# Stores of new keys on ScalarE's queue, forget sums on GpSimd's, temporaries moved, and a softmax that takes the minimum of negated scores

## The chip, the cores and the metric

The kernel runs on one core of a Trainium2 chip. The metric is the time of one execution on the device in microseconds (us). The engines are named as in the profile: PE is TensorE, and PEld its weight loads; DVE is VectorE, ACT ScalarE, POOL GpSimd and SP SyncE. SyncE only issues transfers here; ScalarE and GpSimd issue some between their own instructions. An engine works through its instructions in the order in which they were placed, and an instruction that waits holds all that stand behind it.

## The reference

One inference step of a two-layer trunk for 512 prompt rows and 8 x 16 sample rows (640 rows in all, model width 1024, branch width 2048). Layer 0 is a gMLP layer that the change does not touch. Layer 1 is attention with 16 heads of 128 and a forget gate:

```python
proj = h @ w_in                               # q, k, v, z and 16 forget columns
logf = log_sigmoid(proj[..., 4 * E:] + b_f)
# prompt: causal, for each head
cT = cumsum(logf, axis=1)
s = q @ k.T * scale + cT[query] - cT[key]     # then the causal mask
o = softmax(s) @ v
# sample: the same over 256 cached rows (cache_fox_k, cache_fox_v, cache_fox_logf) and 16 new ones
y = (o * silu(z)) @ w_out
```

After it come an RMS norm, the residual and a gated embedding, as in layer 0. The new k, v and logf rows of prompt and sample are outputs too, in the layout (row, head, channel).

## The kernel before, in words

Products in float32 are made of three products of float32r parts: `split(hi, lo, src)` (line 285) rounds on ScalarE (line 288) and takes the rest on VectorE (line 289), and `mm3` (line 269) issues the three matmuls (lines 271 to 273). The projections of layer 1 use a scheme of seven products for a 2 x 2 block (`seven_products`, line 556): of each product of 12 matmuls, into one of four PSUM banks (`PRJ` and `UZ`), the first is copied out by ScalarE (line 571) and the others are added out by VectorE (lines 562, 573, 575, 578). The left operands are sums of weight blocks that GpSimd builds (line 210), and GpSimd also issues the weights' loads. The right operands are sums of blocks of h that `right_operands` makes on VectorE (lines 426 to 437).

The heads are worked through in pairs p = 0 to 7. While TensorE projects z of pair p and v, k, q of pair p + 1, the attention of pair p is cut into pieces that `interleave(steps, pieces)` (line 356) puts between the matmuls: each matmul step adds an estimated time, and each piece has a due time. The attention pieces use three other banks (`ATT`). The compiler's planner then orders each engine's instructions by a simulated timeline, so that a due time is a wish and not a place; `queued("dve")` ties the instructions inside it behind the last one that was noted in `behind`.

What the pieces do, by the names that matter here:

- `forget_logits` (line 808), `log_forget` (line 820) and `forget_sums` (line 840) make the 16 forget columns, their log sigmoid and its cumulative sums for all heads, once, at the start of the layer. The sums are stored to DRAM (`c_sc` for the prompt, `cs_sc` for the samples) and read back as a row that is spread over 128 partitions: `load_w0(h)` for a head's prompt row (into `SF` or `CST`), `load_mask(i)` for four sample requests.
- `load_k(p, bg, hh)` (line 1039) loads the cached K of a head and four requests into the one buffer `kraw` with four transfers of 1024 pieces of 128 bytes. `turn_k` (line 1051) turns it with four VectorE transposes (line 1055), after which the next load may start; `new_k` adds the new keys. `load_v` loads cached V.
- `prompt_pieces(h)` (line 974): `scores(i)` takes scores of a block of 128 queries, subtracts the forget row, takes the row maximum in the same VectorE instruction (lines 1004 and 1007), negates it (line 1010), and ScalarE takes the Exp (line 1011); then `turn` (line 1022) and `values` (line 1029), whose last step writes y over z (line 1031). `sample_pieces` does the same for four requests (lines 1079 to 1120), its negation in line 1084.
- `store_k(h, tr)` (line 919) transposes a head's new keys on VectorE and stores them with eight transfers in pieces of 128 bytes, on SyncE's queue. It is called from `project_k` when a head's sum is done, for both heads of a pair in close sequence.
- `store_y(p)` (line 1138) stores both heads' y on GpSimd's queue at the end of a pair; the next pair's z is written to the same place, the odd head first.

Before the loop over pairs stand `project_v0`, `project_k0` and `project_q(0)` for the first pair, with the forget gate's pieces and the first loads between them. The forget gate's temporaries lie in one run from the start of `R1` (`tmpa`), over the buffers of turned K (`o_KT`) and raw K (`o_K`).

Of the kernel before, what the change touches and what calls it, by code (L numbers as in the profile page):

```python
# [24 lines left out]
P = 128  # L25
# [32 lines left out]
def hybrid_trunk(tc, x_prompt, x_sample, ck, cv, clf, p_prompt, p_sample, norm_pre, norm_post,  # L58
# [31 lines left out]
    def r1(o, n, p=P):  # L90
        return R1[:p, o:o + n]
# [191 lines left out]
    scale = DH ** -0.5  # L283
# [495 lines left out]
    def tmpa(n, p=P):  # L779
        nonlocal o  # L780
        res = r1(o, n, p)
        o += n
        return res
# [11 lines left out]
    cr = tmpa(256).rearrange("p (t n) -> p t n", t=2)  # L795
# [6 lines left out]
    fx, fa, fe, fl, fu, lft = (tmpa(n) for _ in range(6))  # L802
    lf3 = lft.rearrange("p (t h) -> p t h", t=NT)
    fx3 = fx.rearrange("p (t h) -> p t h", t=NT)
    cT, ex, cS = tmpa(SEQ, H), tmpa(P), tmpa(272)
    assert o <= o_V
# [33 lines left out]
    def forget_sums():  # L840
# [4 lines left out]
        dma(c_sc, cT)  # L845
# [9 lines left out]
        dma(cs_sc, cS)  # L855
# [63 lines left out]
    def store_k(h, tr):  # L919
        nc.vector.transpose(out=tr, in_=both(o_k, h % 2))  # L920
        trv = tr.rearrange("p (c d) -> p c d", d=32)
        for qd in range(4):
            dma(fk_p[0, 0, :, h, qd * 32:(qd + 1) * 32].rearrange("(c j) d -> j c d", j=32), trv[qd * 32:(qd + 1) * 32, :16])
            dma(fk_s[0, :, :, h, qd * 32:(qd + 1) * 32].rearrange("(c b) q d -> (b q) c d", c=4), trv[qd * 32:(qd + 1) * 32, 16:])

    def project_k0():
        ws = weights(2)
        n = TOK - SA
        for h in range(2):
# [4 lines left out]
            nc.vector.tensor_tensor(out=kt[:, SA:], in0=kt[:, SA:], in1=b[:, :n], op=ALU.add)  # L934
# [39 lines left out]
    def prompt_pieces(h):  # L974
# [13 lines left out]
        def scores(i):  # L988
# [12 lines left out]
            init = -3e38  # L1001
            if i:
                m0 = small()
                nc.vector.tensor_tensor_reduce(out=pr[:, :i * P], in0=S[:, :i * P], in1=w0[:, :i * P], scale=1.0, scalar=init,
                                               op0=ALU.subtract, op1=ALU.max, accum_out=m0)
                init = m0
            nc.vector.tensor_tensor_reduce(out=pr[:, d], in0=S[:, d], in1=w1, scale=1.0, scalar=init,
                                           op0=ALU.subtract, op1=ALU.max, accum_out=m)
            nm, sm = small(), small()
            nc.vector.tensor_scalar(out=nm, in0=m, scalar1=-1.0, scalar2=None, op0=ALU.mult)  # L1010
            nc.scalar.activation(out=pr[:, :n], in_=pr[:, :n], func=AF.Exp, bias=nm, accum_out=sm)  # L1011
# [54 lines left out]
    def sample_pieces(p, bg):  # L1066
# [6 lines left out]
        def scores():  # L1073
# [3 lines left out]
            for hh in range(2):  # L1077
                for bl in range(4):
                    nc.tensor.matmul(S[32 * bl:32 * bl + 32, :272], qpads[:, hh, 4 * bg + bl].rearrange("p h q -> p (h q)"),  # L1079
                                     kt[:, hh, bl], start=(hh == 0), stop=(hh == 1))  # L1080
            m, nm, sm, ri = small(), small(), small(), small()
            nc.vector.tensor_tensor_reduce(out=pr[:, :272], in0=S[:, :272], in1=Wc, scale=1.0, scalar=-3e38, op0=ALU.subtract,
                                           op1=ALU.max, accum_out=m)
            nc.vector.tensor_scalar(out=nm, in0=m, scalar1=-1.0, scalar2=None, op0=ALU.mult)
            nc.scalar.activation(out=pr[:, :272], in_=pr[:, :272], func=AF.Exp, bias=nm, accum_out=sm)
# [52 lines left out]
    def store_y(p):  # L1138
        for hh in range(2):
            dma(y_sc[2 * p + hh], y_of(2 * p + hh), nc.gpsimd)  # L1140
# [13 lines left out]
    def attention_pieces(p, step, s1):  # L1154

        s0, t0 = 5, 4
        pieces = sample_times(p, 0, s0) + sample_times(p, 1, s1)
        pieces += [(s0 + 5, lambda: turn_k(p, 1, 0)), (s0 + 5.1, lambda: load_k(p, 1, 1)), (s0 + 17.6, lambda: turn_k(p, 1, 1)),
                   (s0 + 17.7, lambda: new_k(p, 1)), (s0 + 13.5, lambda: load_v(p, 1))]
        for hh in range(2):  # L1160
            pieces += prompt_times(2 * p + hh, t0 + 4 * step * hh, step)
        if p < 7:
            pieces += [(s0 + 17.8, lambda: load_k(p + 1, 0, 0)), (s1 + 13.5, lambda: load_v(p + 1, 0))]
# [11 lines left out]
    def sums_of_h():  # L1175
        sums.append(right_operands((o_P, o_v + 1280, o_V, o_qp, o_z)))

    interleave(project_v0(), [(0.0, forget_logits), (0.1, sums_of_h), (6.0, log_forget)])
    interleave(project_k0(), [(1.0, forget_sums), (4.0, lambda: load_k(0, 0, 0)), (6.0, lambda: load_w0(0)), (6.05, lambda: load_w0(1)), (6.06, lambda: load_mask(0)), (6.1, lambda: load_v(0, 0))])
    split(*quarter(0, 1), sums[0])  # L1180
    nc.gpsimd.memset(r1(o_qp, 512), 0.0)
    interleave(project_q(0), [(0.2, lambda: turn_k(0, 0, 0)), (0.3, lambda: load_k(0, 0, 1)), (12.0, lambda: turn_k(0, 0, 1)),
                              (12.1, lambda: load_k(0, 1, 0)), (12.2, lambda: new_k(0, 0))])
# [49 lines left out]
```

## Time and profile before

| | |
|---|---|
| Time, median of 3 runs | 1314.44 us (1314.06 to 1314.46) |
| The profiled execution's own time | 1318.47 us |
| Its span, first to last instruction | 1316.6 us |
| PE busy | 1286.0 us (98%) |
| DVE, ACT, POOL busy | 970.5 us (74%), 587.8 us (45%), 349.1 us (27%) |
| Mean share of the DMA queue of SyncE (q1) | 35.5% of 16 engines |
| GpSimd's queue (q0), ScalarE's queue (q10) | 13.7%, 1.2% |

Matmuls are pipelined, so that "busy" hides what a slow clock costs; the granted clock (PEclk, 1.00 is full speed) has to be read beside it. The attention layer's projections begin at 531.5 us of the span; the last pair's z projection ends near 1111 us, and the output projection follows. In a timeline row stand the start, the duration (us), engine, line, operation, what is written and read, the number of merged instructions, and in brackets how long the engine was idle before it and what ended that. "SPq" and "ACTq" rows are issues of transfers by SyncE and ScalarE; their duration is the time in which that engine's sequencer was held.

### The profile page before, as it was taken

How to read it: one execution, taken by the hardware profiler on the slowest of the kernel's cores; microseconds unless marked ns; L12 is line 12 of the kernel's file. 1: busy time of each engine (PE TensorE's matmuls, PEld its weight loads, DVE VectorE, ACT ScalarE, POOL GpSimd, SP SyncE). 2: the span in 40 equal slices, each digit the busy share in tenths (PEclk: the TensorE clock that was granted, in tenths of full speed). 3: DMA queues.
4: the chain of work that ended last, by engine and by line, in shares of the span. 5: the costliest groups of instructions: out<-in, count | busy, mean ns of one | idle time of the engine just before them, and what ended most of it. 6: DMA issues, size and time to landing. Idle time of an engine off the chain costs nothing. (4 is left out here: it accounts for less than half of the span.)

```text
span 1316.6 us, 21174 instructions
## 1 busy us (share of the span) xinstructions
PE 1286.0 (98%) x7873; PEld 1147.1 (87%) x7873; DVE 970.5 (74%) x1888; ACT 587.8 (45%) x1062; POOL 349.1 (27%) x322
## 2 busy tenths in 40 slices
PE   9999999999999999998989999999989999999998
PEld 6888999999988888886878999999979998788887
DVE  7744999999844455986858888889879987744643
ACT  5334555444535343453435444544444444535431
POOL 1012454543000100343432444444434530000100
PEclk9999999999999999998999999999989999999999
DMA  6432333232324213457878768677778757742111
GB/s 226 131 108 67 122 119 118 91 99 73 129 96 154 70 49 108 123 112 144 154 148 161 182 160 180 150 167 141 153 117 187 170 118 205 283 140 80 65 57 56
DMA packets 275545, 171.53 MB, mean 130 GB/s; under 512 B 188721, under 2 KB 238689, under 8 KB 275442
## 3 DMA queue, kind: packets, MB, share of 16 engines
q1 hardware_dynamic: 261770, 128.63, 35.5%
q0 software_dynamic: 9760, 36.05, 13.7%
q10 hardware_dynamic: 3912, 5.50, 1.2%
q8 instruction: 62, 1.02, 0.3%
q14 instruction: 41, 0.34, 0.1%
HBM read 148.55 MB, written 21.59 MB: 129 GB/s over the span
## 5 line engine op out<-in xcount | busy, mean ns | idle before, releaser
L271 PE MATMUL pb<-A,W 128*128 128x320 f32 (+1 forms) x752 | 242.4, 322 | 7.2 <-DVE R L578 3.7
L273 PE MATMUL pb<-A,W 128*128 128x320 f32 (+1 forms) x752 | 236.3, 314 | 0.0
L272 PE MATMUL pb<-A,W 128*128 128x320 f32 (+1 forms) x752 | 235.3, 313 | 0.0
L271 PE MATMUL pb<-W,A 128*128 128x512 f32 x520 | 204.9, 395 | 3.5 <-DVE R L562 2.0
L272 PE MATMUL pb<-W,A 128*128 128x512 f32 x520 | 203.7, 392 | 0.0
L273 PE MATMUL pb<-W,A 128*128 128x512 f32 x520 | 203.3, 393 | 0.1
L289 DVE TENSOR_TENSOR W<-RAW,W 128x1024 fp32r<-128x1024 f32 (+1 forms) x126 | 144.8, 1150 | 74.2 <-ACT W L288 71.8
L288 ACT ACTIVATE W<-RAW 128x1024 fp32r<-128x1024 f32 (+1 forms) x126 | 119.9, 952 | 94.8 <-PE pb L273 48.3
L271 PEld LDWEIGHTS pb<-A,W 128*128 128x128 f32 x752 | 143.4, 191 | 9.3 <-DVE R L578 4.0
L272 PEld LDWEIGHTS pb<-A,W 128*128 128x128 f32 x752 | 143.3, 191 | 1.2 <-issue 0.9
L273 PEld LDWEIGHTS pb<-A,W 128*128 128x128 f32 x752 | 143.0, 190 | 0.8 <-issue 0.4
L271 PEld LDWEIGHTS pb<-W,A 128*128 128x128 f32 x520 | 98.1, 189 | 23.9 <-ACT A L288 2.3
L301 POOL TENSOR_TENSOR SML<-SML 128x1 f32<-128x1 f32 x25 | 18.5, 740 | 376.9 <-DVE SML L299 372.2
L271 PE MATMUL pb<-tbf,W 128*128 128x320 f32 x360 | 117.5, 326 | 0.1
L273 PEld LDWEIGHTS pb<-W,A 128*128 128x128 f32 x520 | 97.9, 188 | 20.6 <-DVE A L289 0.5
L272 PEld LDWEIGHTS pb<-W,A 128*128 128x128 f32 x520 | 98.0, 188 | 19.6
L210 POOL TENSOR_TENSOR sff<-RAW 128x512 f32<-128x512 f32 x46 | 60.8, 1322 | 202.8 <-DVE W L289 97.6
L272 PE MATMUL pb<-tbf,W 128*128 128x320 f32 x360 | 112.2, 312 | 0.0
L273 PE MATMUL pb<-tbf,W 128*128 128x320 f32 x360 | 112.0, 311 | 0.0
L562 DVE TENSOR_TENSOR R<-R,pb 128x320 f32<-128x320 f32 x184 | 86.6, 479 | 20.1 <-PE pb L273 13.6
L289 DVE TENSOR_TENSOR A<-R,A 128x640 fp32r<-128x640 f32 (+1 forms) x42 | 34.5, 854 | 61.9 <-ACT A L288 61.9
L1011 ACT ACTIVATE R<-R,SML 128x128 f32<-128x128 f32 (+1 forms) x64 | 35.7, 558 | 92.5 <-DVE SML L1010 91.9
(267 smaller groups left out, 2875.2 us busy)
## 6 DMA issues: line engine op xcount, KB each, us to landing
RAW<-in_fox_w_in POOLq DMA_DIRECT2D x46, 512.0 KB, 7.2
RAW<-in_gmlp_w_in SPq DMA_DIRECT2D x40, 512.0 KB
R<-in_cache_fox_v SPq DMA_DIRECT2D x32, 512.0 KB
R<-in_cache_fox_k SPq DMA_DIRECT2D x128, 128.0 KB
RAW<-in_gmlp_w_out SPq DMA_DIRECT2D x16, 512.0 KB
RAW<-in_ple_w_gate SPq DMA_DIRECT2D x16, 512.0 KB
RAW<-in_fox_w_out SPq DMA_DIRECT2D x16, 512.0 KB
R<-in_fox_w_in POOLq DMA_DIRECT2D x14, 512.0 KB, 7.7
```

Source lines behind the costliest of these rows:

```text
L210: nc.gpsimd.tensor_tensor(out=o, in0=a, in1=b, op=op)
L271: nc.tensor.matmul(out, lh, rh, start=start, stop=False)
L272: nc.tensor.matmul(out, lh, rl, start=False, stop=False)
L273: nc.tensor.matmul(out, ll, rh, start=False, stop=stop)
L288: nc.scalar.activation(out=hi, in_=src, func=AF.Copy)
L289: nc.vector.tensor_tensor(out=lo, in0=src, in1=f(hi), op=ALU.subtract)
L301: nc.gpsimd.tensor_tensor(out=q, in0=t, in1=mhalf, op=ALU.pow)
L562: behind["dve"] = nc.vector.tensor_tensor(out=into(i, j), in0=a, in1=b, op=ALU.add)
L1011: nc.scalar.activation(out=pr[:, :n], in_=pr[:, :n], func=AF.Exp, bias=nm, accum_out=sm)
```

## The change

The forget row is added to negated scores and the minimum is taken (the scale of q is negative now); the Exp gets scale -1 and the minimum as its bias, and the instruction that negated the maximum falls away, in `scores` of prompt and sample. The new keys are stored over ScalarE's queue. The sums of the forget gate are stored, and the first rows loaded, over GpSimd's queue. Its temporaries move to other buffers, so that raw K's buffer is free from the start of the layer and the first load of cached K is issued in `project_v0`; the order and due times of the first pieces change with it. y is stored head by head, the even head's at a due time inside the pair. The prompt pieces begin at 3.2 instead of 4, and in pairs 0 to 6 follow in steps of 4.7 instead of 4.8. `project_k0` notes its VectorE sum in `behind`.

```diff
-    scale = DH ** -0.5
+    scale = -DH ** -0.5
...
-    cr = tmpa(256).rearrange("p (t n) -> p t n", t=2)
+    cr = r1(o_PTs + 96, 256).rearrange("p (t n) -> p t n", t=2)
...
-    fx, fa, fe, fl, fu, lft = (tmpa(n) for _ in range(6))
+    fx, fa, fe, fl, fu, lft = (r1(o_V + 1280 + z * n, n) for z in range(6))
...
-    cT, ex, cS = tmpa(SEQ, H), tmpa(P), tmpa(272)
-    assert o <= o_V
+    cT, ex, cS = r1(o_PT + 288, SEQ, H), r1(o_PT + 800, P), r1(o_V + 1760, 272)
+    assert o <= o_K and o_PT + 288 >= o_P + 1280 and o_PTs + 96 >= o_qp + 1280
...
-        dma(c_sc, cT)
+        dma(c_sc, cT, nc.gpsimd)
...
-        dma(cs_sc, cS)
+        dma(cs_sc, cS, nc.gpsimd)
...
         for qd in range(4):
-            dma(fk_p[0, 0, :, h, ...], trv[qd * 32:(qd + 1) * 32, :16])
-            dma(fk_s[0, :, :, h, ...], trv[qd * 32:(qd + 1) * 32, 16:])
+            dma(fk_p[0, 0, :, h, ...], trv[qd * 32:(qd + 1) * 32, :16], nc.scalar)
+            dma(fk_s[0, :, :, h, ...], trv[qd * 32:(qd + 1) * 32, 16:], nc.scalar)
...
-            nc.vector.tensor_tensor(out=kt[:, SA:], in0=kt[:, SA:], in1=b[:, :n], op=ALU.add)
+            behind["dve"] = nc.vector.tensor_tensor(out=kt[:, SA:], in0=kt[:, SA:], in1=b[:, :n], op=ALU.add)
...
-            init = -3e38
+            init = 3e38
             if i:
                 m0 = small()
                 nc.vector.tensor_tensor_reduce(out=pr[:, :i * P], in0=S[:, :i * P], in1=w0[:, :i * P], scale=1.0, scalar=init,
-                                               op0=ALU.subtract, op1=ALU.max, accum_out=m0)
+                                               op0=ALU.add, op1=ALU.min, accum_out=m0)
...
-            nm, sm = small(), small()
-            nc.vector.tensor_scalar(out=nm, in0=m, scalar1=-1.0, scalar2=None, op0=ALU.mult)
-            nc.scalar.activation(out=pr[:, :n], in_=pr[:, :n], func=AF.Exp, bias=nm, accum_out=sm)
+            sm = small()
+            nc.scalar.activation(out=pr[:, :n], in_=pr[:, :n], func=AF.Exp, scale=-1.0, bias=m, accum_out=sm)
...
-    def store_y(p):
-        for hh in range(2):
-            dma(y_sc[2 * p + hh], y_of(2 * p + hh), nc.gpsimd)
+    def store_y(h):
+        dma(y_sc[h], y_of(h), nc.gpsimd)
...
-        s0, t0 = 5, 4
+        s0, t0 = 5, 3.2
...
         if p < 7:
-            pieces += [(s0 + 17.8, lambda: load_k(p + 1, 0, 0)), (s1 + 13.5, lambda: load_v(p + 1, 0))]
+            pieces += [(s1 + 18, lambda: store_y(2 * p)), (s0 + kb + 0.2, lambda: load_k(p + 1, 0, 0)), (s1 + 13.5, lambda: load_v(p + 1, 0))]
...
-    interleave(project_v0(), [(0.0, forget_logits), (0.1, sums_of_h), (6.0, log_forget)])
-    interleave(project_k0(), [(1.0, forget_sums), (4.0, lambda: load_k(0, 0, 0)), (6.0, lambda: load_w0(0)), (6.05, lambda: load_w0(1)), (6.06, lambda: load_mask(0)), (6.1, lambda: load_v(0, 0))])
+    interleave(project_v0(), [(0.0, forget_logits), (2.0, log_forget), (2.1, sums_of_h), (9.0, forget_sums),
+                              (9.1, lambda: load_w0(0, nc.gpsimd)), (1.0, lambda: load_k(0, 0, 0))])
+    interleave(project_k0(), [(11.0, lambda: turn_k(0, 0, 0)), (11.1, lambda: load_k(0, 0, 1)), (0.0, lambda: load_w0(1, nc.gpsimd)), (0.1, lambda: load_mask(0, nc.gpsimd)), (6.0, lambda: load_v(0, 0))])
     split(*quarter(0, 1), sums[0])
     nc.gpsimd.memset(r1(o_qp, 512), 0.0)
-    interleave(project_q(0), [(0.2, lambda: turn_k(0, 0, 0)), (0.3, lambda: load_k(0, 0, 1)), (12.0, lambda: turn_k(0, 0, 1)),
-                              (12.1, lambda: load_k(0, 1, 0)), (12.2, lambda: new_k(0, 0))])
+    interleave(project_q(0), [(8.0, lambda: turn_k(0, 0, 1)),
+                              (8.1, lambda: load_k(0, 1, 0)), (12.2, lambda: new_k(0, 0))])
...
-        pieces = attention_pieces(p, 4.8, 26.0) + next_keys(p + 1, 34.0, 46.2)
+        pieces = attention_pieces(p, 4.7, 26.0) + next_keys(p + 1, 34.0, 46.2)
...
-        store_y(p)
+        store_y(2 * p + 1)
```

The sample scores change like the prompt's.

More of the change, by code (lines that the diff above doesn't have):

```diff
@@ L922, in store_k @@
         for qd in range(4):
-            dma(fk_p[0, 0, :, h, qd * 32:(qd + 1) * 32].rearrange("(c j) d -> j c d", j=32), trv[qd * 32:(qd + 1) * 32, :16])
-            dma(fk_s[0, :, :, h, qd * 32:(qd + 1) * 32].rearrange("(c b) q d -> (b q) c d", c=4), trv[qd * 32:(qd + 1) * 32, 16:])
+            dma(fk_p[0, 0, :, h, qd * 32:(qd + 1) * 32].rearrange("(c j) d -> j c d", j=32), trv[qd * 32:(qd + 1) * 32, :16], nc.scalar)
+            dma(fk_s[0, :, :, h, qd * 32:(qd + 1) * 32].rearrange("(c b) q d -> (b q) c d", c=4), trv[qd * 32:(qd + 1) * 32, 16:], nc.scalar)
     def project_k0():
@@ L1004, in scores @@
                 nc.vector.tensor_tensor_reduce(out=pr[:, :i * P], in0=S[:, :i * P], in1=w0[:, :i * P], scale=1.0, scalar=init,
-                                               op0=ALU.subtract, op1=ALU.max, accum_out=m0)
+                                               op0=ALU.add, op1=ALU.min, accum_out=m0)
                 init = m0
             nc.vector.tensor_tensor_reduce(out=pr[:, d], in0=S[:, d], in1=w1, scale=1.0, scalar=init,
-                                           op0=ALU.subtract, op1=ALU.max, accum_out=m)
-            nm, sm = small(), small()
-            nc.vector.tensor_scalar(out=nm, in0=m, scalar1=-1.0, scalar2=None, op0=ALU.mult)
-            nc.scalar.activation(out=pr[:, :n], in_=pr[:, :n], func=AF.Exp, bias=nm, accum_out=sm)
+                                           op0=ALU.add, op1=ALU.min, accum_out=m)
+            sm = small()
+            nc.scalar.activation(out=pr[:, :n], in_=pr[:, :n], func=AF.Exp, scale=-1.0, bias=m, accum_out=sm)
             if i == 3 and h + 2 < 14:
@@ L1080, in scores @@
                                      kt[:, hh, bl], start=(hh == 0), stop=(hh == 1))
[L1081 to L1085, printed above, removed]
+            m, sm, ri = small(), small(), small()
+            nc.vector.tensor_tensor_reduce(out=pr[:, :272], in0=S[:, :272], in1=Wc, scale=1.0, scalar=3e38, op0=ALU.add,
+                                           op1=ALU.min, accum_out=m)
+            nc.scalar.activation(out=pr[:, :272], in_=pr[:, :272], func=AF.Exp, scale=-1.0, bias=m, accum_out=sm)
             if 2 * p + bg < 15:
@@ L1154, in attention_pieces @@
     def attention_pieces(p, step, s1):
-        s0, t0 = 5, 4
+        s0, t0 = 5, 3.2
         pieces = sample_times(p, 0, s0) + sample_times(p, 1, s1)
-        pieces += [(s0 + 5, lambda: turn_k(p, 1, 0)), (s0 + 5.1, lambda: load_k(p, 1, 1)), (s0 + 17.6, lambda: turn_k(p, 1, 1)),
-                   (s0 + 17.7, lambda: new_k(p, 1)), (s0 + 13.5, lambda: load_v(p, 1))]
+        ka, kb = 5, 17.6
+        pieces += [(s0 + ka, lambda: turn_k(p, 1, 0)), (s0 + ka + 0.1, lambda: load_k(p, 1, 1)), (s0 + kb, lambda: turn_k(p, 1, 1)),
+                   (s0 + kb + 0.1, lambda: new_k(p, 1)), (s0 + 13.5, lambda: load_v(p, 1))]
         for hh in range(2):
```

## The prediction, made before the changed kernel ran

> **What bounds the kernel now.** I read the page first: one core, one span, and shares of the engines.
>
> ```profile
> span 1316.6 us, 21174 instructions
> PE 1286.0 (98%) x7873; PEld 1147.1 (87%) x7873; DVE 970.5 (74%) x1888; ACT 587.8 (45%) x1062; POOL 349.1 (27%) x322
> PEclk9999999999999999998999999999989999999999
> ```
>
> TensorE is the bound: it is busy for 98% and the change takes no matmul away. So the change can only win what TensorE loses in the attention layer, which is all that it touches. The second view is the table by windows of 20 us; these are the windows from 560 us on in which TensorE's time, the first number behind the width, is under 20.
>
> ```profile
> core 0: us, PE busy (x) PEld busy (x) DVE busy (x) ACT busy (x) POOL busy (x), PEclk, DMA share, GB/s
> 560.00:580.00 20.00, 19.05 (x118) 17.86 (x118) 18.67 (x28) 11.41 (x17) 9.17 (x8) 1.00 0.44 104
> 580.00:600.00 20.00, 17.45 (x112) 15.43 (x110) 10.66 (x20) 6.34 (x9) 7.42 (x8) 0.98 0.82 160
> 600.00:620.00 20.00, 17.91 (x84) 12.90 (x85) 17.02 (x48) 8.98 (x19) 7.87 (x8) 0.85 0.69 121
> 620.00:640.00 20.00, 18.18 (x140) 16.65 (x139) 17.47 (x49) 9.13 (x20) 7.96 (x8) 1.00 0.62 112
> 660.00:680.00 20.00, 16.24 (x122) 14.81 (x121) 12.52 (x33) 6.75 (x14) 7.96 (x9) 1.00 0.74 160
> 680.00:700.00 20.00, 17.52 (x116) 16.21 (x115) 14.19 (x40) 9.08 (x21) 7.05 (x7) 0.91 0.76 134
> 700.00:720.00 20.00, 18.51 (x144) 17.34 (x143) 16.32 (x47) 9.34 (x20) 6.92 (x7) 1.00 0.82 173
> 960.00:980.00 20.00, 15.02 (x91) 13.74 (x91) 11.89 (x29) 5.52 (x11) 6.52 (x5) 0.83 0.58 84
> 1100.00:1120.00 20.00, 17.97 (x113) 15.20 (x111) 14.29 (x42) 7.86 (x16) 0.47 (x2) 1.00 0.72 189
> 1120.00:1140.00 20.00, 19.16 (x115) 14.50 (x115) 15.27 (x43) 11.74 (x23) 0.00 (x0) 1.00 0.96 356
> ```
>
> Ten windows lack 200 - 177.01 = 22.99 us of TensorE. Behind three of the stalls the granted clock is about half as well, which a third view, windows cut to those stretches, prices: what is lost is the width times what the clock lacks.
>
> ```profile
> 601.20:606.20 5.00, 4.19 (x15) 3.79 (x16) 5.00 (x12) 2.40 (x4) 2.29 (x3) 0.50 0.48 89
> 688.00:691.50 3.50, 3.50 (x16) 3.50 (x15) 2.93 (x8) 0.85 (x2) 2.50 (x3) 0.51 0.07 8
> 972.90:979.40 6.50, 6.50 (x26) 5.75 (x27) 6.50 (x13) 2.54 (x7) 5.48 (x5) 0.59 0.39 60
> ```
>
> 5.00 x 0.50 = 2.5, 3.50 x 0.49 = 1.7, 6.50 x 0.41 = 2.7: another 6.9 us. The pot is 22.99 + 6.9 = 29.9 us. Fourth, TensorE's timeline names the longest stalls in brackets with the releaser, and VectorE's, ScalarE's and SyncE's timelines what lay behind that releaser.
>
> ```profile
> 572.84 0.42 PE L271 MATMUL pb<-A,W 128*128 128x320 f32 x1 [0.60 <-ACT A L288]
> 601.18 0.64 PE L271 MATMUL pb<-A,W 128*128 128x320 f32 x1 [3.73 <-DVE R L578]
> 687.03 0.42 PE L271 MATMUL pb<-A,W 128*128 128x320 f32 x1 [2.48 <-DVE R L562]
> 972.90 0.69 PE L271 MATMUL pb<-W 128*128 128x384 f32 x1 [4.98 <-DVE SML L1007]
> 1112.01 0.47 PE L271 MATMUL pb<-W,A 128*128 128x512 f32 x1 [1.96 <-DVE R L562]
> ...
> 598.51 0.29 DVE L994 TENSOR_TENSOR R<-sff,CST 128x128 f32<-128x128 f32 x1 [7.93 <-DMA sff<-c_sc]
> 663.91 1.43 DVE L1055 STREAM_TRANSPOSE R<-R 128x256 f32<-128x256 f32 x4 [4.40 <-DMA out<-R]
> 686.49 0.49 DVE L562 TENSOR_TENSOR R<-R,pb 128x320 f32<-128x320 f32 x1 [3.93 <-DMA y_sc<-R]
> 946.12 1.42 DVE L1055 STREAM_TRANSPOSE R<-R 128x256 f32<-128x256 f32 x4
> 969.03 1.42 DVE L1055 STREAM_TRANSPOSE R<-R 128x256 f32<-128x256 f32 x4 [8.11 <-DMA R<-in_cache_fox_k]
> ...
> 1105.86 0.74 ACT L288 ACTIVATE A<-R 128x640 fp32r<-128x640 f32 x1 [8.17 <-DMA R<-y_sc]
> ...
> 592.82 8.77 SPq L124 DMA_DIRECT2D R<-in_cache_fox_k  x4
> 930.33 2.46 SPq L124 DMA_DIRECT2D R<-in_cache_fox_k  x4
> 932.89 17.58 SPq L124 DMA_DIRECT2D out<-R  x16
> 951.61 8.31 SPq L124 DMA_DIRECT2D R<-in_cache_fox_k  x4
> 1078.20 8.47 SPq L124 DMA_DIRECT2D out<-R  x16
> ```
>
> The pattern: VectorE takes its work in order and stands before a transfer (the forget sums' first row at 598.51, the cached K at 663.91 and 969.03, the stored y at 686.49); the sums that empty the projections' banks (L562, L578) are queued behind it, and TensorE runs out of banks. At 930 to 960 the cause can be read off SyncE: four loads of cached K take 2.46 us to issue; the 16 stores of new K then hold SyncE for 17.58 us; the next four loads begin at 951.61, need 8.31 us, and land at 969.03.
>
> **The change, part by part.** The profiled execution took 1318.47 us (span 1316.6 and 1.87 around it), 4.03 us above the median of the runs, 1314.44. The sum is made against 1318.47 and the 4.03 taken off.
>
> Forget sums through GpSimd's queue, temporaries moved, logs ahead of the sums of h, first cache loads early. L994 waited for a row that could be stored only after the sums, late in the K projection, and whose load left SyncE's queue shortly before 592.82. The sums now belong into the V projection, which ends some 20 us before 590, where L994 began to wait. The stall of 3.73, its follower of 0.81 in the next window (2.55 + 2.09 = 4.64 with the rest of those two windows) and the half clock's 2.5 go: -7.1. What is late next: VectorE does the logs before the sums of h, whose last split (the row of 0.60 at 572.84) feeds project_q(0), and GpSimd, which builds the weights' left operands (L210), now stands before a transfer's landing at each of its loads. No row shows that wait on GpSimd. Its ends: nothing, if both fill idle time, or the 3.73 of the like stall at 601.18 once more; I take +1.5, nearer to nothing, since VectorE is the only full engine there (18.67 of 20) and the logs are no added work. The first V load now waits for the stored sample sums; no stall row above names a V load, so 0.
>
> Cached K of the first pair. With the temporaries out of its buffer, its load starts before the K projection instead of at 592.82, and each later turn follows. The 1.82 of 620:640 goes: -1.8; if the loads are still late nothing is won.
>
> Stores of new K over ScalarE's queue. SyncE loses 128 issues (eight for each of 16 heads), and the load at 951.61 could leave at once when its buffer is free. Its landing took 969.03 - 951.61 = 17.4 us, of which 8.31 were issue; with an issue like the 2.46 at 930.33 it lands some 6 us earlier, and some 4 more for an earlier start (the VectorE turn that frees the buffer ends at 946.12 + 1.42 = 947.5). The wait of 8.11 is covered: 4.98 + 2.7 = -7.7. For the three windows from 660 to 720, 3.76 + 2.48 + 1.49 = 7.73 and the half clock's 1.7, 9.4 in all, a turn that waits (663.91) began it and a late y store (686.49) ended it; I take two thirds, -6.3. The last two windows, 2.03 + 0.84 = 2.87, hang on y loads queued behind cached K; half, -1.4. Their ends: nothing, and all of it. The first of those ends is the rival of the full DMA engines below.
>
> What ScalarE pays.
>
> ```profile
> L124 SPq DMA_DIRECT2D out<-R x185: 315/486/5832, 134.0 to 1313.2; - x185
> 927.00:950.00 23.00, 23.00 (x172) 21.93 (x171) 19.78 (x47) 10.95 (x19) 8.90 (x10) 1.00 0.73 131
> 578.19 0.31 PE L271 MATMUL pb<-tbf,W 128*128 128x320 f32 x1
> 581.57 0.31 PE L273 MATMUL pb<-tbf,W 128*128 128x320 f32 x1
> ...
> L1010 DVE TENSOR_SCALAR SML<-SML x64: 117/147/160, 600.2 to 1163.9; 128x1 f32<-128x1 f32 x64
> L1084 DVE TENSOR_SCALAR SML<-SML x16: 141/153/155, 627.5 to 1139.1; 128x1 f32<-128x1 f32 x16
> ```
>
> A pair's 16 issues cost 16 x 0.486 = 7.8 us if the queue takes them, up to the 17.58 above if it blocks. Behind them stand the copies of each first product out of its bank (L571), the weights' splits and the Exp. Cover: ScalarE is busy for 10.95 of the 23 us around the stores, so 18.7 with them; and four banks of 12 matmuls at (581.57 - 578.19)/23 = 0.147 us each, 1.76 a product, let TensorE run 3 x 1.76 = 5.3 us on. If all issues stand in front of one copy, 7.8 - 5.3 = 2.5 us show per pair; at 17.58 it would be 12.3; if the order interleaves them, 0. Below nothing is excluded, since the gain on SyncE is counted above. I take +1.0 for each of seven pairs, +7: nearest to the cheap end, because the issues alone leave ScalarE 4 us free of 23 and the stores no longer stand behind loads in one queue.
>
> Minimum of negated scores: 64 x 0.147 + 16 x 0.153 = 11.9 us of VectorE go, and one hop before each Exp. The sign sits in a constant that the split of q's weights multiplies anyway. TensorE does not wait for the Exp in any of the five rows above, so 0; with VectorE at 19.78 of 23 it could be a few us, and its absence costs nothing. y head by head: the same two stores of each pair, the even one earlier; counted in the 1.7 and 7.73 above, else 0; the cover is the three products before the odd head's old y is overwritten. Prompt pieces 0.8 us earlier and steps of 4.7 instead of 4.8: 0, since they shift pieces within a TensorE that is full. Bounds for the shift: one lost or won stall like 1112.01's, +-2.
>
> Sum: -7.1 + 1.5 - 1.8 - 7.7 - 6.3 - 1.4 + 7 = -15.8. 1318.47 - 15.8 = 1302.7; less 4.03: 1298.7, say 1299.
>
> **The rivals.**
>
> Full DMA engines. K loads and K stores wait for the same 16 engines, not for SyncE. For it: the engines' share stands at 0.73 around the stores. Against it: at 0.73 they aren't full, the share falls to 0.58 in the window of the longest stall, and the same 16 stores took 8.47 us at 1078.20. The stalls of 660 to 720, 960 and 1100 stay, ScalarE is hardly stopped (2 in all): -7.1 + 1.5 - 1.8 + 2 = -5.4, 1309. The Trainium skill, DMA: Bandwidth & Descriptors, Issuing engines are not separate DMA queues, speaks for this one: it says that DMAs of all issuing engines share the same DMA engines, so a second issuer saves only its own issue time, usually little beside the transfer. By that rule 1309, by the row of 17.58 us of issue 1299; I side with the row.
>
> ScalarE in the way, which ends slower. All 16 issues come out in a row before the copy of project_q's first product. Each pair then shows 2.5 us, and at the ratio of 601.18 (2.5 of half clock to 3.73 of stall) 1.7 more: 7 x 4.2 = 29.4 in place of 7. 1298.7 + 22.4 = 1321. It decides from (15.8 + 7)/7 = 3.3 us per pair on. For it: ScalarE takes its queue in order, and a wait of one issue holds all behind it. Against it: 18.7 of 23.
>
> Startup turned round. The logs delay the sums of h by as much as they win, and the later gains are lost to ScalarE as above at 2.2 us a pair: -1.8 - 15.4 + 15.4, about 1313, no change.
>
> **How the numbers follow.** 0.2% is 2.6 us, about what can be told from no change. Forecast 0.60, with a range of its own from 1289 (ScalarE's 7 and a third of the middle stalls won) to 1308; full DMA engines 0.16; ScalarE in the way 0.16; startup turned round 0.08. Faster is the first two, 0.76; same 0.08; slower 0.16. The range goes from 1288, where the pot less 3.5 us is won, to 1316, which leaves ScalarE's case and little else out.
>
> **What would show it.** Right: no stall before L994's first row; K loads of four in under 5 us each time; no wait of VectorE over 3 us for cached K; windows 580 to 720 and 960 to 980 full, at clock 1.00. The K stores stand in ScalarE's queue at about 0.5 us each, and L571 follows within 5 us. Wrong: ScalarE rows of stores over 1 us, TensorE waiting for L571, L288 or L562 once a pair, GpSimd's L210 late near 570, or cached K landing as late as before with SyncE idle.

## The result and the profile after

The changed kernel takes **1365.18 us** (median; 1364.44 to 1366.79) against 1314.35 us for the kernel before on the same chip: ratio 1.0387, 95% interval 1.0374 to 1.0401. It is 51 us slower; 1299 was forecast. Two of the runs below have one execution each in a slow state (1589.89 and 3237.12 us); their medians are those of the others. The page of the changed kernel:

```profile
span 1362.7 us, 21092 instructions
PE 1285.8 (94%) x7873; PEld 1152.9 (85%) x7873; DVE 969.3 (71%) x1808; ACT 582.6 (43%) x1062; POOL 356.0 (26%) x327
```

TensorE's busy time is the same to 0.2 us, and the span is 46 us longer: TensorE waits. The view of waits, TensorE's own, from 500 us on (engine, line, who ended the wait; us in total, times, longest):

```profile
PE pb L1112 <- ACT R L1107: 60.1, 7, 11.7
PE pb L843 <- DVE R L836: 5.0, 1, 5.0
PE pb L271 <- DVE R L898: 3.2, 1, 3.2
PE pb L998 <- DVE SML L1007: 0.2, 1, 0.2
```

None of the stalls of before is left (L578, L562 and L1007 at 601, 687, 973 and 1112), and one new wait, once a pair, is twice the old pot: TensorE stands before L1112 of `gate`, the last step of a sample piece, until ScalarE has made the copy of L1107. Behind each of the seven stalls the clock is half again. The windows cut to these stretches, the first, the fifth and the last of seven:

```profile
665.50:670.50 5.00, 4.98 (x28) 4.98 (x29) 4.64 (x11) 3.83 (x8) 1.92 (x2) 0.69 0.18 67
981.20:986.50 5.30, 5.26 (x25) 5.26 (x25) 4.27 (x10) 3.53 (x7) 2.20 (x2) 0.55 0.17 64
1135.60:1140.00 4.40, 4.40 (x19) 4.40 (x20) 3.19 (x7) 3.23 (x6) 0.57 (x1) 0.55 0.20 76
```

Width times missing clock comes to 15.6 us over the seven. ScalarE's bill is so 60.1 + 15.6 = 75.7 us, 10.8 a pair. What ScalarE did is read off its timeline; here the pair whose stall is the longest (start, duration, engine, line, operation, number, idle time and what ended it):

```profile
960.55 3.98 ACTq L122 DMA_DIRECT2D out<-R  x8
...
964.63 1.56 ACTq L122 DMA_DIRECT2D CST<-c_sc  x1
...
966.29 14.33 ACTq L122 DMA_DIRECT2D out<-R  x8
980.72 0.47 ACT L1107 ACTIVATE R<-pb,SML 128x256 f32<-128x256 f32 x1 [15.32 <-DMA out<-R]
981.09 0.43 ACT L571 ACTIVATE R<-pb 128x320 f32<-128x320 f32 x1
...
981.24 0.69 PE L1112 MATMUL pb<-CST,R 128*128 128x128 f32 x2 [11.73 <-ACT R L1107]
```

The first head's eight stores take 3.98 us, the second head's 14.33; L1107 and L571 stand behind them, and at 981.24 TensorE goes on. A row for all 128 stores of the kernel (shortest, median and longest issue in ns) says that a single issue is as a rule still short:

```profile
L122 ACTq DMA_DIRECT2D out<-R x128: 322/498/2737, 572.8 to 1134.5; - x128
```

Eight issues of 0.498 us are 4.0 us. The other 10 of the 14.33 us are of two kinds. One is a wait ahead of an issue for another transfer to land, and the trace's semaphore records say for which. SyncE's and ScalarE's transfers report their landing on eight semaphores in turn; the next transfer on a semaphore is issued only when the one before on it has landed, whichever engine had issued it. In this pair (times in us, "landed" is the last of the 16 reports):

```
store issued   by ScalarE    earlier transfer on its semaphore    issued    landed
971.12         2nd head      store of the 1st head                962.99    971.10
973.00         2nd head      first half of cached V, SyncE        963.30    972.23
978.22         2nd head      store of the 1st head                963.53    978.19
979.27         2nd head      second half of cached V, SyncE       963.79    979.25
```

Three of the four leave 0.02 to 0.03 us after the landing (the other first had to wait for the issue before it, which ended at 972.96). Between the eight issues lie 4.4 us of such waits. The other kind lies inside the issues: four of them are long (1.72, 2.74, 1.84 and 1.92 us), so that the eight hold ScalarE for 9.8 us. From 600 us on, the 112 stores of the seven pairs hold it for 70.9 us in issues and 39.6 in the gaps between them; 35.1 of these gaps end with such a landing. The Trainium skill, Perfetto Trace Analysis, DMA Instruction — HWDGE (DVE, Sync), says that such a row starts when all semaphores are satisfied and then holds a wait for the lock of the descriptor generator and the generation itself, so that gap and row are two different things; the gaps agree, but no run here shows what fills the long rows.

### The profile page after: what moved, and what is told of

It reads as the page before. It is cut to its first block, busy times and chain, and to the rows that moved or that the text cites. A ratio compares the mean times of both kernels' runs of the same rounds, so it can differ in the third digit from the quotient of the medians.

```text
span 1362.7 us, 21092 instructions
## 1 busy us (share of the span) xinstructions
PE 1285.8 (94%) x7873; PEld 1152.9 (85%) x7873; DVE 969.3 (71%) x1808; ACT 582.6 (43%) x1062; POOL 356.0 (26%) x327
## 4 chain that ended last, share of the span: by engine, by line
PE 45%; DMA 8%; DVE 4%; issue 1%; SPq 1%; ACT 1%; ACTq 0%; DVEq 0%
PE pb L271 12%; PE pb L273 12%; PE pb L272 12%; DMA R<-in_cache_fox_v 5%; PE pb L1028 2%; DMA out<-R 2%; PE pb L1021 1%; PE pb L1078 1%; PE pb L1105 1%; DVE W L289 1%; SPq L124 1%; PE pb L1102 1%; DVE R L1054 1%; PE pb L906 0%; PE pb L1112 0%
## 5 line engine op out<-in xcount | busy, mean ns | idle before, releaser
L271 PE MATMUL pb<-A,W 128*128 128x320 f32 (+1 forms) x752 | 246.2, 327 | 3.2 <-DVE R L898 3.2
L273 PE MATMUL pb<-A,W 128*128 128x320 f32 (+1 forms) x752 | 237.7, 316 | 0.0
L272 PE MATMUL pb<-A,W 128*128 128x320 f32 (+1 forms) x752 | 237.5, 316 | 0.0
L289 DVE TENSOR_TENSOR W<-RAW,W 128x1024 fp32r<-128x1024 f32 (+1 forms) x126 | 157.1, 1248 | 73.8 <-ACT W L288 70.9
L271 PE MATMUL pb<-W,A 128*128 128x512 f32 x520 | 204.6, 394 | 0.7 <-ACT A L288 0.7
L271 PEld LDWEIGHTS pb<-A,W 128*128 128x128 f32 x752 | 145.5, 193 | 4.3 <-DVE R L898 3.6
L272 PEld LDWEIGHTS pb<-A,W 128*128 128x128 f32 x752 | 145.3, 193 | 0.1
L273 PEld LDWEIGHTS pb<-A,W 128*128 128x128 f32 x752 | 144.8, 193 | 0.0
L271 PE MATMUL pb<-tbf,W 128*128 128x320 f32 x360 | 115.7, 321 | 0.0
L271 PEld LDWEIGHTS pb<-W,A 128*128 128x128 f32 x520 | 98.0, 189 | 20.6 <-ACT A L288 1.1
L562 DVE TENSOR_TENSOR R<-R,pb 128x320 f32<-128x320 f32 x184 | 86.4, 477 | 10.0 <-PE pb L273 9.0
L573 DVE TENSOR_TENSOR R<-R,pb 128x320 f32<-128x320 f32 x46 | 22.0, 478 | 81.0 <-ACT R L571 80.6
```

What stands on the lines that cost most here:

```text
L271: nc.tensor.matmul(out, lh, rh, start=start, stop=False)
L272: nc.tensor.matmul(out, lh, rl, start=False, stop=False)
L273: nc.tensor.matmul(out, ll, rh, start=False, stop=stop)
L289: nc.vector.tensor_tensor(out=lo, in0=src, in1=f(hi), op=ALU.subtract)
L562: behind["dve"] = nc.vector.tensor_tensor(out=into(i, j), in0=a, in1=b, op=ALU.add)
L573: nc.vector.tensor_tensor(out=u2, in0=m1, in1=o, op=ALU.add)
```

## Experiments

Ratios are to the kernel before, run on the same chip in the same group. S is the theory of the semaphores, F that of full DMA engines, I that of issue time alone.

### All of new K's stores back on SyncE

```diff
-            dma(fk_p[...], trv[..., :16], nc.scalar)
-            dma(fk_s[...], trv[..., 16:], nc.scalar)
+            dma(fk_p[...], trv[..., :16])
+            dma(fk_s[...], trv[..., 16:])
```

> The changed kernel with the stores of new K back on SyncE's queue; all else stays. Three theories of the 7 stalls (60.1 us of TensorE waiting for L1107, some 15 us of half clock behind them). S: SyncE's and ScalarE's transfers share eight completion semaphores in the compiled program, so a store issue on ScalarE waits until the transfer eight before it has landed, and holds ScalarE for that time. F: the DMA engines are full in these stretches, so that stores and loads are late whoever issues them. I: 16 issues of about 0.5 us each are too much for ScalarE. S and I expect the seven stalls gone, 1365 - 75 = 1290, and up to 1300 if a load of cached K is late again behind the stores. F expects stalls of like size at other places in the same seven stretches: 1340 or more. All three expect the two stalls of the start (3.24 and 5.02) to stay.

1295.44 us, ratio 0.984 (0.9824 to 0.9855), so F alone falls: all bytes still move. SyncE's timeline:

```profile
917.56 15.36 SPq L124 DMA_DIRECT2D out<-R  x16
933.02 1.02 SPq L124 DMA_DIRECT2D R<-in_cache_fox_v  x2
934.13 21.28 SPq L124 DMA_DIRECT2D R<-in_cache_fox_k  x8
```

The 15.36 us for 16 stores are still there, as the 17.58 were before. Here only loads stand behind them, and TensorE loses 3.02 us at 952.08. Nearly all of the 15.36 us lies inside the issues (14.6 us, up to 3.31 each); a semaphore's landing is waited for in 0.1 us of it.

### The kernel before, with these stores alone on ScalarE

The two lines above put into the kernel before, nothing else.

> The kernel before with nothing changed but the queue of the new K's stores, ScalarE's for SyncE's. S and I expect seven stalls once a pair, behind the second head's stores, of 5 to 12 us each: 1314 + 75 less up to 20 for the earlier loads of cached K, so 1370 to 1390. F expects the time of before within 10 us, since the same transfers go through the same engines.

1370.66 us, ratio 1.0407 (1.039 to 1.0425). The waits of TensorE (L1114 and L1109 are this kernel's L1112 and L1107):

```profile
PE pb L1114 <- ACT R L1109: 54.0, 8, 10.1
```

This one edit is the loss: 55 us of time.

### Cached V on GpSimd's queue

```diff
-            dma(vv[...], cv[...])
+            dma(vv[...], cv[...], nc.gpsimd)
```

> The changed kernel with the loads of cached V on GpSimd's queue, which has completion semaphores of its own; the new K's stores stay on ScalarE's. The same bytes move. In the compiled program of the changed kernel two of the second head's eight stores wait for the two V loads. S expects the second head's batch to be held no longer for V, only for loads of cached K and the first head's stores: stalls of 0 to 5 us in place of 5.5 to 11.7, a time of 1310 to 1340. F and I expect the seven stalls as before, 1360 to 1370.

1362.33 us, ratio 1.0346 (1.0331 to 1.0361): a miss for S, since the stalls for L1107 shrank only to 55.8 us. ScalarE's timeline in the same pair:

```profile
964.63 1.18 ACTq L122 DMA_DIRECT2D out<-R  x1
965.85 12.70 ACTq L122 DMA_DIRECT2D out<-R  x7
978.66 0.47 ACT L1107 ACTIVATE R<-pb,SML 128x256 f32<-128x256 f32 x1 [13.74 <-DMA out<-R]
```

By the semaphore records none of these eight stores waits for a landing: whatever was ahead on its semaphore had landed before the engine came to it. The issues themselves take 13.3 of the 13.9 us, up to 2.56 each. Over the seven pairs the gaps that end with a landing fall from 35.1 to 5.5 us, and the issues grow from 70.9 to 98.7; from the first store of a pair to its last ScalarE is held for 113.9 us in all, where it was 118.1. The hold stayed and moved from the gaps into the issue rows. So the shared semaphores are not the cause by themselves: with most of these waits gone, ScalarE is held nearly as long.

### New K's stores on GpSimd's queue

`nc.gpsimd` in place of `nc.scalar`.

> The changed kernel with the new K's stores on GpSimd's queue. S: ScalarE is free, GpSimd is held instead, for the landing of weight loads (7.5 us each) and of its own stores, and what it builds of the weights (L210) comes late; with the slack that GpSimd had (26% busy) 1290 to 1330. F: like the changed kernel, 1350 or more. I: GpSimd's issues cost about what its other transfers cost, 0.55 to 0.77 us, 16 of them 10 us a pair of an engine that is idle most of the time: 1290.

1310.24 us, ratio 0.9954 (0.9939 to 0.9968). GpSimd's transfers have semaphores of their own. An issue costs more there, but none is long; the second view has the median us to landing at the end of its rows:

```profile
L122 POOL DMA_DIRECT2D out<-R x128: 561/659/743, 573.5 to 1084.4; - x128
...
out<-R POOLq DMA_DIRECT2D x56, 64.0 KB, 4.6
out<-R POOLq DMA_DIRECT2D x56, 16.0 KB, 4.3
```

It pays with many small stalls: 2.98 us at 607, 20 of 0.3 to 1.0, and the startup's 3.39. GpSimd also builds the weights' operands, which may be why; that is not shown.

### The same issues, small stores

```diff
-            dma(fk_p[...], trv[..., :16], nc.scalar)
-            dma(fk_s[...], trv[..., 16:], nc.scalar)
+            dma(fk_p[...][:, :1], trv[..., :1], nc.scalar)
+            dma(fk_s[...][:, :1], trv[..., 16:17], nc.scalar)
```

> The changed kernel, with each of ScalarE's 16 stores of a pair cut to one piece of 128 bytes per partition (before 16 and 4); the rest of new K is not written. As many issues, on the same engine, at the same place. Theory S (ScalarE's issue waits for an earlier transfer to land): small stores land in some 4 us instead of 10 to 14, so ScalarE's issues shrink from 14.3 us for 8 (at 966.29) to about 4 to 6, TensorE's stalls for the copy at L1107 (60.1 us in 7) fall below 15, and the time is 1292 to 1310. Theory I (ScalarE pays 16 issues of 0.5 us each, and that is what delays it): nothing changes in the issues, the stalls stay above 45 and the time above 1345. Theory F (the bytes of these stores hold up other transfers): also about 1295, but then the kernel with the stores on SyncE, 1295.4 with all the bytes, has no explanation.

1360.58 us, ratio 1.0347 (1.0331 to 1.0362): a clear miss for S as I had put it. ScalarE's timeline in the same pair:

```profile
966.38 12.95 ACTq L122 DMA_DIRECT2D out<-R  x8
979.43 0.47 ACT L1107 ACTIVATE R<-pb,SML 128x256 f32<-128x256 f32 x1 [14.24 <-DMA out<-R]
```

The semaphore records say why: two of these stores left at 972.71 and 978.06, and the halves of V on their semaphores had landed at 972.69 and 978.04. A store of 4 KB, issued at 966.38, landed at 977.52: 11.1 us, while V (1 MB) and two weight blocks (1 MB, GpSimd's) were in flight. The landing's time has little to do with a transfer's own size here.

### First head's stores on ScalarE, second head's on SyncE

```diff
-            dma(fk_p[...], trv[..., :16], nc.scalar)
+            dma(fk_p[...], trv[..., :16], None if h % 2 else nc.scalar)
```

(and `fk_s` the same).

> The changed kernel, with the first head's 8 stores of each pair left on ScalarE and the second head's 8 on SyncE. Theory S: the first head's stores are issued in about 4 us now (3.98 for 8 at 960.55), and the 14.3 us belongs to the second head's, which waited for the first's to land; on SyncE they hold up only loads. TensorE's stalls for L1107 fall from 60.1 to under 12, and the time is 1293 to 1308. Theory I: half of the issues stay, so about half of the loss: stalls of 25 to 35, 1325 to 1340.

1304.82 us, ratio 0.9908 (0.9879 to 0.9937). TensorE has no wait for L1107 at all. ScalarE's timeline and SyncE's at the same place:

```profile
929.97 3.99 ACTq L122 DMA_DIRECT2D out<-R  x8
934.06 1.53 ACTq L122 DMA_DIRECT2D CST<-c_sc  x1
935.69 0.47 ACT L1107 ACTIVATE R<-pb,SML 128x256 f32<-128x256 f32 x1 [0.86 <-PE pb L273]
...
934.01 17.16 SPq L124 DMA_DIRECT2D out<-R  x8
```

The second head's stores hold SyncE for 17.16 us now, and the copy at L1107, which stood behind them, runs at 935.69. What they hold up is the cached K behind them: two stalls before L271, 11.8 us.

### The second head's stores later on ScalarE

```diff
+        if h < 2 or h % 2 == 0:
+            send_k(h, tr)
+        else:
+            late.append((h, tr))
...
+        pieces += [(26.0, lambda p=p: turn_v(p + 1, 0)), (27.0, lambda p=p: turn_v(p + 1, 1)), (48.5, send_late)]
```

`send_k` is the loop of eight stores, all still on ScalarE.

> The changed kernel with all 16 stores of a pair still on ScalarE, whole, but the second head's 8 issued 11.5 steps (some 18 us) later, after the copy at L1107 instead of ahead of it. Issues, bytes and queue are the same; only what the second head's stores stand behind, and ahead of, differs. Theory S, mended after the small stores (an issue on ScalarE or SyncE waits for the landing of the transfer some eight ahead, and a landing takes 8 to 14 us there whatever the size, as all engines are full of V, weights and cached K): the first head's stores and the loads have landed by then, the second head's 8 issues take 3.5 to 6 us, TensorE's 60.1 us of stalls for L1107 fall under 12: 1293 to 1308. Rival: the wait forms again further on, behind the next pair's transfers: stalls of 20 to 40, 1315 to 1340. Theory I (the issue time itself): above 1340.

1325.23 us, ratio 1.0077 (1.0056 to 1.0097): the rival's time. Same issues, bytes and queue; 40 us are back. The wait forms again before another copy:

```profile
ACT R L1034 <- DMA out<-R: 32.7, 6, 6.8
...
PE pb L1039 <- ACT R L1034: 18.4, 6, 5.8
```

### An eighth of V, and with small stores as well

```diff
-            dma(vv[:, ...], cv[...])
+            dma(vv[:16, ...], cv[...][:16])
```

> The changed kernel, all 16 stores whole and on ScalarE, with cached V loaded for 16 of 128 partitions alone (an eighth of its bytes; the rest of V's tile keeps what it held). Theory S with full engines: the landings that ScalarE waits for (the first head's stores 963.53 to 978.19, V 963.79 to 979.25) are long because V's 1 MB and the weights' 1 MB fill the DMA engines then; with 0.9 MB less they land within 8 us, the stalls for L1107 fall from 60.1 to 10 to 30 us, 1305 to 1335. Rival: the stores' own pieces of 128 bytes take that long: stalls above 45, over 1350.

> The changed kernel with both cuts: each of ScalarE's 16 stores of a pair one piece of 128 bytes per partition, and an eighth of V's bytes (new K's rest not written, the rest of V's tile old). As many issues in the same places. Theory S with full engines: little is left in flight, so landings are quick; the stalls for L1107 (60.1; 56.2 with small stores alone, 34.0 with an eighth of V alone) fall under 15, the time to 1295 to 1315. Theory I (issue time of 16 times 0.45): stalls stay near 34, 1330 or more.

1338.95 us (1.0183; 1.0153 to 1.0213) and 1330.33 us (1.0123; 1.0105 to 1.014). The waits of TensorE in the one and in the other:

```profile
PE pb L1112 <- ACT R L1107: 34.0, 7, 7.0
```

```profile
PE pb L1112 <- ACT R L1107: 28.6, 7, 6.4
```

V's bytes are the largest part that was found: 26 of the 60 us go with them, 4 with the stores' bytes, 31 with both; 28.6 stay. S had forecast 10 to 30 and under 15, and missed; I's bound for the last time, 1330, was met. It isn't the issue time of 0.43 us, though. In the last kernel the longest stall stands here:

```profile
957.30 0.69 PE L1112 MATMUL pb<-CST,R 128*128 128x128 f32 x2 [6.36 <-ACT R L1107]
```

TensorE asked for the copy at 957.30 - 6.36 = 950.94, and the first store was issued at 941.98: 16 issues of 0.43 and c_sc's of 0.83 are 7.7 us and fit into the 8.96. The second head's eight took 10.04 all the same: 2.0 for the landing of the c_sc row (issued 945.71, landed 956.33), and two issues of 2.83 and 1.85 us, while GpSimd's weight blocks were in flight (944.1 to 955.9). The row and the stores behind it land only after the second block has. No run changes the weight loads, so that they are the rest is a rival left untested, and why such an issue is long stays open.

### Minimum, attention's steps, startup, GpSimd's stores, each alone

Each time the kernel before with one part of the change: the minimum of negated scores; the earlier prompt pieces, steps of 4.7 and y by heads; the startup's order with temporaries and GpSimd's stores; the two stores on GpSimd's queue without the rest.

> The kernel before with the minimum of negated scores alone: the negation on VectorE (72 instructions of 0.165 us, 11.9 us in all) is gone, all else stays. If VectorE's time is hidden there, as forecast: 1312 to 1317. Rival: the negation lies in the chain scores, maximum, exponential that TensorE waits for, and the gain is a good part of 11.9 us: 1303 to 1309.

> The kernel before with the attention's part of the change alone: first prompt piece at 3.2 for 4, step 4.7 for 4.8, y stored head by head. The forecast priced it at 0 (2 either way): 1312 to 1317. Rival: the earlier pieces take away some of the stalls at L1021 and L1028 (6.0 and 5.9 us in the kernel with the minimum alone) and are a good part of the 19 us between 1314.4 and 1295.4: 1300 to 1308.

> The kernel before with the startup's part of the change alone: forget gate's temporaries moved, its sums stored by GpSimd, the new order of its steps and of the first loads; maximum, attention's steps, y and new K's stores as before. If the 19 us come from here: 1293 to 1300. Rival: the parts give it only together (stalls at L1021 and L1028 further on stay): 1303 to 1312.

> The kernel before with the two stores of the forget sums on GpSimd's queue alone. Forecast's first term, 7.1 us for the stall at 601.18: 1306 to 1310. Rival: the row is late anyway, or the stall moves to the next wait: 1312 to 1316.

| part alone | us | ratio, 95% |
|---|---|---|
| minimum | 1313.16 | 0.9987 (0.9975 to 0.9999) |
| attention's steps and y | 1312.98 | 0.9987 (0.9974 to 0.9999) |
| startup | 1305.74 | 0.9938 (0.9916 to 0.996) |
| stores on GpSimd alone | 1324.01 | 1.0061 (1.004 to 1.0082) |

Minimum and attention are worth 0.13% each at the median, under what can be told from no change. Startup brings 9.0 us, within the rival's 1303 to 1312. The GpSimd queue alone costs 9.2: both of its forecasts (1306 to 1310, and 1312 to 1316) missed, and the stall meant to go grew. TensorE's timeline there, and VectorE's:

```profile
608.45 0.69 PE L271 MATMUL pb<-W 128*128 128x384 f32 x1 [7.93 <-DVE SML L1007]
...
604.59 0.29 DVE L994 TENSOR_TENSOR R<-sff,CST 128x128 f32<-128x128 f32 x1 [8.31 <-DMA sff<-c_sc]
```

The row comes later than before (604.59 for 598.51), not earlier: its store leaves at 594.05 for 588.43 and takes 6.4 us to land for 3.4. In the startup part alone it comes later still, at 609.56. What that part wins is won elsewhere; the section on the prediction shows where.

### The first load of cached K and x_sc's last store

Three tries on the kernel with the stores on SyncE: the load due at step 8.0 of V's projection, at 0.0 and at 2.5 of K's, and then tied behind the store by an order of its own:

```diff
                     dma(x_sc[t], x1[t])
+                    behind["x"] = behind["sp"]
...
+    def first_k():
+        with queued("x"):
+            load_k(0, 0, 0)
```

> The kernel with all of new K's stores on SyncE (1295.4), and the first load of cached K due at step 8.0 instead of 1.0 of V's first projection. If the startup stall of 3.25 us at 551.66 (clock .83 from 540 to 560, some 3 us more) is owed to this load standing in SyncE's line ahead of the last store of x_sc, it goes: 1288 to 1293. Rival: the load is then late for its own transposes before the first pair, or the wait stays with another releaser: 1294 to 1298.

> The kernel with all of new K's stores on SyncE (1295.4), and the first load of cached K moved from V's first projection to the start of K's. The later step alone did not move it (it was issued at 535.49 again, ahead of the last store of x_sc). Theory: VectorE's 7.01 us wait ahead of L432 is for that store, whose buffer it overwrites; with the store in front, the stall of 3.2 us for L898 and the half clock behind it go: 1288 to 1292. Rival: another thing holds L432 or the cached K is then late: 1294 to 1298.

> The kernel with the stores on SyncE (1295.4), the first load of cached K now behind the last store of x_sc in SyncE's compiled order (step 2.5 of K's first projection). Theory: the stall of 3.2 to 3.6 us at 551 for L898 goes, with its half clock of some 3 us: 1288 to 1292. Rival: L432 waits for something else, or the first transposes of cached K are late in turn: 1294 to 1298.

> The kernel with the stores on SyncE (1295.4), the first load of cached K tied behind the last store of x_sc by an order of its own (two runs with a later due step had left it ahead: issued at 535.74, the store at 541.04). Theory: x_sc's last store is then issued near 538.7, as before, lands near 542, VectorE's L432 no longer waits 7 us, the stall of 3.2 to 3.6 us for L898 goes with its half clock: 1287 to 1292. Rival: L432 waits on, or the first transposes of cached K come late in turn: 1293 to 1297.

1297.54, 1296.98, 1293.48 and 1291.94 us (ratio of the last 0.9827, 0.9806 to 0.9847). The first three changed nothing that was meant to change: the planner kept the load in front (the third said "now behind", and that was not so). SyncE's timeline of the third and of the tied one, with VectorE's row behind it:

```profile
535.74 5.20 SPq L124 DMA_DIRECT2D R<-in_cache_fox_k  x4
541.04 3.09 SPq L124 DMA_DIRECT2D x_sc<-R  x1
```

```profile
524.96 13.65 SPq L124 DMA_DIRECT2D x_sc<-R  x3
538.79 6.94 SPq L124 DMA_DIRECT2D R<-in_cache_fox_k  x4
...
542.37 1.48 DVE L432 TENSOR_TENSOR R<-A 128x1280 f32<-128x1280 f32 x1
```

Tied, VectorE's L432 no longer waits (6.99 us in the changed kernel, at 549.01, for that store to land), and TensorE's stall of 3.2 to 3.6 us near 551 is gone. In time nothing is shown: the intervals of the four overlap, and the ratio is 0.9827 beside 0.984 without the tie. It has the lowest median of all: the change with its stores left on SyncE, and this tie.

### SyncE with the second head's stores later

> As the run before last of this group (stores on SyncE, first load of cached K after x_sc), and the second head's stores 11.5 steps later, behind the loads of cached K. Theory S: SyncE's 15.4 us for 16 stores at 917.56 no longer stand ahead of cached K's loads, the stall of 3.02 us at 952.08 with its half clock goes: 2 to 5 us under that kernel, 1285 to 1290. Rival: no wait of TensorE hangs on it, within 1.5 us of that kernel.

The edit is the one of the run on ScalarE above; the kernel that the text names is the second try with the load, 1296.98. 1299.35 us, ratio 0.9877 (0.9858 to 0.9896): no gain, and the stall for cached K grew to 3.90 at 957.10. SyncE's timeline shows that the second head's stores still stood ahead of the loads of cached K:

```profile
928.04 13.70 SPq L124 DMA_DIRECT2D out<-R  x8
941.84 18.51 SPq L124 DMA_DIRECT2D R<-in_cache_fox_k  x8
```

So the case that was meant wasn't tried.

## Why the prediction was wrong

**The step that failed is the price of ScalarE's issues**, "16 x 0.486 = 7.8 us if the queue takes them, up to the 17.58 above if it blocks", taken at +1.0 a pair. It measured 10.8 a pair (75.7 in seven), near the far end of 12.3; taking the edit out of the changed kernel gives 1365.18 - 1295.44 = 69.7 us back. The row of 17.58 us was read as SyncE's capacity to issue, which a second queue would add to. It was a hold, and it moved with the stores: from an engine behind which only transfers stand to one behind which TensorE's next copy stands. By the trace before, 14.3 of the 17.58 us are the 16 issues (up to 2.91 each) and 2.6 a wait on a shared semaphore. The cheap end had little for it: over the seven pairs SyncE's rows of 16 stores add up to 88.1 us, 12.6 a pair against 7.8, and only the last pair's 8.47 is near it. "The stores no longer stand behind loads in one queue" was the false reason: on the shared semaphores they do, and where they don't, with V on GpSimd, the issues themselves grow. Why an issue grows stays open.

**The rival "ScalarE in the way"** had the mechanism ("a wait of one issue holds all behind it"), the half clock and the sign; its 4.2 a pair was too small by 6.6, and its copy was L571 where L1107 came first. The point from which it decides, 3.3 a pair, was far exceeded, and its sign, stores of over 1 us in ScalarE's queue, was there: 17 of the 112.

**Full DMA engines** was rejected as a rival, and its times were wrong (1309, and stalls that stay). Yet what it says is part of the cause: without most of V's bytes 26 of the 60 us went, and with V on another queue, its bytes whole, 4.3 did. That the engines are full is not shown: their mean share is 0.80 from 960 to 980. What share the weight loads have was not tried. By the rule of the Trainium skill, DMA: Bandwidth & Descriptors, Issuing engines are not separate DMA queues, a second issuer saves only issue time; the runs agree that nothing was saved, and add that a second issuer can lose what stands behind its issues: 1315.6 to 1370.7 us for the edit alone, beside 1295.4 on SyncE with the rest.

**The gains.** Without ScalarE's term the sum was 1291.7 us; the kernel with the stores on SyncE takes 1295.4, and 1291.9 with the startup's load tied. That the size is right is luck, since the terms are not. Terms 1 and 2, -7.4 with the exposure, were not won: from 540 to 640 us TensorE lacks 7.41 us before and 7.74 with the stores on SyncE, and the half clock costs 3.4 and 5.1 beside. The stall of 601.18 stands at 612.14 now, because the sums come later, not earlier. VectorE's copy of the sums (L844) and its first use of the row, before and with the stores on SyncE, and TensorE's stall:

```profile
586.56 0.67 DVE L844 COPY R<-pb 16x512 f32<-16x512 f32 x1
598.51 0.29 DVE L994 TENSOR_TENSOR R<-sff,CST 128x128 f32<-128x128 f32 x1 [7.93 <-DMA sff<-c_sc]
```

```profile
600.15 0.67 DVE L844 COPY R<-pb 16x512 f32<-16x512 f32 x1
610.49 0.31 DVE L994 TENSOR_TENSOR R<-sff,CST 128x128 f32<-128x128 f32 x1 [5.27 <-DMA sff<-c_sc]
...
612.14 0.69 PE L271 MATMUL pb<-W 128*128 128x384 f32 x1 [3.38 <-DVE SML L1007]
```

"The sums now belong into the V projection" was read off the due times; the planner didn't place them there. (In the changed kernel itself L844 stands at 583.68, behind the stall of 5.0 us for the logs, and TensorE lacks 8.72 us from 540 to 640.) The -15.4 credited to stores leaving SyncE isn't theirs: with them on SyncE the middle stalls go too, and the one for cached K shrinks from 4.98 to 3.02. It is the startup part that takes the middle stalls away, and from there its 9.0 us come; by which step it does so was not traced. Its windows alone, where before lacked 3.76, 2.48 and 1.49 and the half clock cost 1.7:

```profile
660.00:680.00 20.00, 20.00 (x150) 19.15 (x149) 17.72 (x41) 9.03 (x17) 8.06 (x9) 1.00 1.01 197
680.00:700.00 20.00, 19.63 (x142) 17.91 (x140) 19.22 (x47) 9.87 (x20) 8.01 (x7) 1.00 0.70 115
700.00:720.00 20.00, 20.00 (x152) 18.02 (x154) 18.70 (x45) 10.60 (x23) 11.40 (x11) 1.00 0.86 186
```

**"0, since they shift pieces within a TensorE that is full"** was wrong as an argument. The page's line of TensorE with attention's steps alone, and with everything but ScalarE's stores:

```profile
PE 1279.4 (98%) x7873; PEld 1145.4 (87%) x7873; DVE 972.6 (74%) x1888; ACT 586.3 (45%) x1062; POOL 356.4 (27%) x322
```

```profile
PE 1270.9 (98%) x7873; PEld 1144.2 (89%) x7873; DVE 961.1 (74%) x1808; ACT 589.5 (46%) x1062; POOL 352.6 (27%) x327
```

The same 7873 matmuls, 6.6 and 15.1 us less busy than before's 1286.0. The clock isn't the reason: the granted mean is 0.993 before and 0.993 and 0.992 there. The pot of 29.9 was thus not all that could be won: "busy" held more, though what it held is not shown. The Trainium skill, Perfetto Trace Analysis, Identifying the Most-Contended Engine, says that matmul occupancy is no good measure of how near a kernel is to its limit, because pipelined matmuls look smaller in the trace; these lines agree that it moves with the work unchanged. That attention's steps alone did not show it in the time (1312.98) goes with a stall of 5.38 us at 666 that the startup part takes away; the parts were not run in pairs.

**Startup exposure**, +1.5 for GpSimd, came in the changed kernel through another engine: VectorE's L432 waited 7 us for x_sc's store behind the early load (3.2 at TensorE), and TensorE waited 5.0 for the log chain (L836), which the forecast did not name. The minimum at 0 held; y at 0 was seen only together with attention's steps.

## What to carry to other kernels

Before moving a transfer to another engine's queue, ask how long that engine will be held by it, not only how long a single issue usually takes: a row of 16 issues that lasts twice as long as 16 medians is a hold, in the gaps or inside the issues, and the hold moves with the issues to everything that stands behind them. Put stores that may be held on the engine that has nothing to do but transfers. Taking away one wait (V's semaphores) is not enough when another takes its place; compare the whole hold. Check in the compiled order that a moved piece has moved. And a TensorE that is 98% busy may still have more to give than its idle time.

## What was not expected of the hardware

- A store of 4 KB took 11.1 us to land beside 2 MB of V and weights; 64 KB, issued 963.53, took 14.7. From GpSimd the same stores landed in 4.6 and 4.3 us (64 and 16 KB, medians).
- An issue by ScalarE that waits for no landing took up to 4.29 us (with V on GpSimd's queue, 810.49), where 0.43 to 0.50 is usual, while weight blocks and V were in flight; GpSimd's own stores never took over 0.743.
- After each stall of 5 to 12 us the granted clock was about half for some 5 us: 15.6 us on top of 60.1.
